# A hybrid encoder layer on one core: weight sums a slot behind their loads, three tiles moved off A's place, one hand-written order for stages 3 to 5

## The chip, the core and the metric

The kernel runs on one core of a Trainium2 chip. The core has TensorE (PE, matrix products; PEld is its weight load), VectorE (DVE), ScalarE (ACT), GpSimd (POOL) and SyncE (SP), which here only issues DMAs; POOL issues DMAs too, beside arithmetic. The metric is the device time in microseconds of one execution; lower is better.

## What is computed

One layer over a prompt of 2048 tokens and a sample of 64 tokens, 1024 features, all in 32-bit floats:

```python
def trunk_layer(x, mk, mv, conv_buf, C0, n0, m0, ff_buf, p):
    y, conv_new, C, n, m = token_mixer(rms_norm(x, p['norm_mix_pre']), conv_buf, C0, n0, m0, ...)
    x = x + rms_norm(y, p['norm_mix_post'])
    y = memory_attend(rms_norm(x, p['norm_mem_pre']), mk, mv, p['w_mq'], p['w_mo'])
    x = x + rms_norm(y, p['norm_mem_post'])
    y, ff_new = conv_ffn(rms_norm(x, p['norm_ffn_pre']), ff_buf, p['w_up'], p['ffn_conv_w'], p['w_down'])
    x = x + rms_norm(y, p['norm_ffn_post'])
    return x, conv_new, C, n, m, ff_new

def memory_attend(xn, mk, mv, w_q, w_o):          # 4 heads of 256, 256 memory tokens
    q = (xn @ w_q).reshape(B, T, MEM_HEADS, MEM_HD)
    s = jnp.einsum('bthd,bmhd->bhtm', q, mk) * (MEM_HD ** -0.5)
    o = jnp.einsum('bhtm,bmhd->bthd', jax.nn.softmax(s, axis=-1), mv).reshape(B, T, D_MODEL)
    return o @ w_o

def conv_ffn(xn, ff_buf, w_up, ffn_conv_w, w_down):   # d_ff = 2816
    up, ff_new = causal_dwconv(xn @ w_up, ff_buf, ffn_conv_w)
    a, g = jnp.split(up, 2, axis=-1)
    return (jax.nn.gelu(g) * a) @ w_down, ff_new
```

`token_mixer` is one input projection, a gated short convolution beside an mLSTM with four heads, and one output projection.

## The kernel before

The kernel splits each 32-bit matrix into a high and a low half (`split`, L102 on ScalarE and L103 on VectorE; `split_g`, L108 and L109, the same with a gain) and makes each product of three matrix products (`mm3`, L116 to L118). `self.dma` (L72) issues on SP, `self.store` (L75) on POOL. Five stages follow one another:

- Stage 1 makes the input projection, stage 2 the mLSTM and the output projection. For each 128 tokens, `post` (L558 to L568) takes the norm of the result, adds the residual from the tile `xt2` and stores the row as `x1d` from one of two tiles `yn2`. Those three tiles and `cn`, the mLSTM's memory, lie in the pool `p2w`.
- Stage 3 is the attention. First a fold: it multiplies the query weights with the memory's keys (products `pA`) and the memory's values with the output weights (`pB`), which gives the matrices A and B, each as two halves; their pools take the place that stage 2's pools leave. Then come 16 chunks of 128 tokens: transposes of `x1` (L1073), scores, softmax, output, `post`, which stores `x2d`, and `x2_T`, which transposes the normed result for stage 4 (L1229). Beside that `sums` prepares stage 4's weights in 44 slots: a slot loads four pieces of `w_up` of 128 KB into a tile `sums` (three buffers, shared with other raw loads), makes four additions or subtractions on VectorE (L1141 to L1144) and stores the tile as `wsd` with 512 KB. Slots are called at up to three points per chunk.
- Stage 4 is the up projection with its convolution and gate, 3 passes of 22 units, in a scheme that saves one product in eight with the sums of the weights; the result goes to memory as `hd`.
- Stage 5 is the down projection. The 2816 rows of weights are taken in six parts (`PARTS`), and each part goes through all tokens in blocks of 256: load `hr<-hd`, split to `hh` (two buffers each), products `y`, addition to `acc` (L1580). In the last part, the norm and the residual `xt<-x2d` (L562 to L568) follow the additions of each chunk of 128, and two stores `out_y` of 256 KB from SP. There a chunk's L568 and its stores come only after the squares of the next chunk (`hold`).

Where nothing is said, a scheduler sets each engine's order from the program's order and its own estimates; `manual_schedule` takes an engine out of this and gives it the program's order. Before, PE was so ordered in all stages, SP in the chunks of stage 3 and in stage 4, ACT, DVE and POOL in the fold and in the last part of stage 5. SP in stage 5 was the scheduler's. All DMAs that an engine issues stand in its row in one order: what stands behind one that waits, waits too.

Of the kernel before, what the change touches and what calls it, by code (L numbers as in the profile page):

```python
# [7 lines left out]
F32 = mybir.dt.float32  # L8
F32R = mybir.dt.float32r
AF = mybir.ActivationFunctionType  # L10
ALU = mybir.AluOpType
# [3 lines left out]
P = 128  # L15
D = 1024
# [17 lines left out]
NB = 352  # L34
NPASS = T // (2 * NB)
PARTS = [3, 3, 4, 4, 4, 4]
CG = dict(mix=0, mem=8, kv=16, ffn=24, mnw=32, cw=36, fw=48)
# [29 lines left out]
class Prog:  # L67
# [68 lines left out]
    def build(self):  # L136
        tc, nc = self.tc, self.nc
        with ExitStack() as es:
# [41 lines left out]
            self.phase2()  # L180
            self.phase3()
            self.phase4()
            self.phase5()

# [543 lines left out]
    def phase2(self):  # L728
        tc, nc, a = self.tc, self.nc, self.a
        V = nc.vector  # L730
        with ExitStack() as es:
# [11 lines left out]
            wk.tile([P, 16], F32, name="padw")  # L743
            yns = [wp.tile([P, D], F32, name="yn2%d" % i) for i in range(2)]
            gb = wp.tile([P, D], F32, name="gb2")
            xt_ = wp.tile([P, D], F32, name="xt2")
            wo1 = wp.tile([P, 2, 4, D], F32R, name="wo1")
            wo = lambda part, k, sl: (self.wo0(part, k) if k < 4 else wo1[:, part, k - 4])[:, sl]
            cn = {16: wp.tile([P, H, VW], F32, name="cn_s"), 0: wp.tile([P, H, VW], F32, name="cn_p")}

# [227 lines left out]
    def phase3(self):  # L978
# [8 lines left out]
        with ExitStack() as es:  # L987
            es.enter_context(tc.manual_schedule(engines={self.pe}))
            py_ = self.pool(es, "p3py", bufs=3, space=PSUM)
            with ExitStack() as es0:  # L990
                zw = self.wop.tile([P, 7168], F32R, tag="w", name="zw")
                raw4 = self.wop.tile([P, D], F32, tag="w7", name="raw4")
# [62 lines left out]

            es.enter_context(tc.manual_schedule(engines={mybir.EngineType.SP}))
            zq = self.zq = self.pool(self.qes, "zq", side="right")
# [72 lines left out]
            def sums():  # L1130

                KH = KT // 2
                for f in range(NF):
                    for q in range(2):
                        t = self.rawp.tile([P, 4, 2 * P], F32, tag="raw", name="sums", bufs=3)
                        for i, j in ((0, f), (1, NF + f)):
                            src = a["w_up"][j].rearrange("p (two k) c -> p two k c", two=2)[:, :, 2 * q:2 * q + 2]
                            for h in range(2):
                                self.dma(t[:, i + 2 * h], src[:, h].rearrange("p k c -> p (k c)"))
                        a11, a21, a12, a22 = (t[:, i] for i in range(4))  # L1140
                        V.tensor_tensor(out=a22, in0=a21, in1=a22, op=ALU.add)  # L1141
                        V.tensor_tensor(out=a21, in0=a11, in1=a21, op=ALU.subtract)
                        V.tensor_tensor(out=a11, in0=a22, in1=a11, op=ALU.subtract)
                        V.tensor_tensor(out=a12, in0=a12, in1=a11, op=ALU.subtract)  # L1144
                        self.store(self.wsd[f, :, :, q * 2 * P:(q + 1) * 2 * P], t)
                        yield
# [88 lines left out]
    def phase4(self):  # L1235
# [14 lines left out]
        with ExitStack() as es:  # L1250
            es.enter_context(tc.manual_schedule(engines={self.pe, mybir.EngineType.SP}))
            left = self.pool(es, "p4l")
# [47 lines left out]
            def w_split(w, n):  # L1300
                if w is None:
                    return
                if n == "wd":
                    o = left.tile([P, 2, KH, P], F32R, tag="wd", name="wd", bufs=1)
                else:
                    o = first.pop(n, None)
                    if o is None:
                        o = w_op(n, 2 if n == "wc" else 1)
                self.split(o[:, 0], o[:, 1], w.r[n])
                w.o[n] = o  # L1310
# [102 lines left out]
            w = w_load(0, ("wb",), tk.w)  # L1413
            w_split(w, "wa")
            t_split(0, tk, "B11", tk.r["R11"])
            t_split(0, tk, "B21", tk.r["R21"])
            v = head1(0, w, tk.o)
            t_adds(tk)
            t_split(0, tk, "T2", tk.X)
            w_split(w, "wb")  # L1420
# [78 lines left out]
    def phase5(self):  # L1499
        tc, nc, a = self.tc, self.nc, self.a  # L1500
        V = nc.vector
        with ExitStack() as es:
            es.enter_context(tc.manual_schedule(engines={self.pe}))
            ac0 = self.pool(es, "p5a")
# [38 lines left out]
            def need(i):  # L1543
                if i < len(work) and i not in hs:
                    pi, t0 = work[i]
                    hs[i] = load_h(f0s[pi], PARTS[pi], t0)
            ws = {0: load_down(0, 0, PARTS[0])}
            need(0)
            held = None
            tail = None  # L1550
            for i, (pi, t0) in enumerate(work):
                last = pi == len(PARTS) - 1
                if t0 == groups[3] and pi + 1 < len(PARTS):
                    ws[pi + 1] = load_down(pi + 1, f0s[pi + 1], PARTS[pi + 1])
                if i == len(PARTS):
# [4 lines left out]
                need(i)  # L1560
                need(i + 1)
                h = hs.pop(i)
                for j in range(t0 // P, (t0 + min(2 * P, T - t0) + P - 1) // P):
# [117 lines left out]
```

## Time and profile before

| | us |
|---|---|
| median of 3 runs (lowest, highest) | 2924.99 (2923.73, 2928.92) |
| the profiled execution | 2930.46 |
| its span, first to last instruction | 2928.8 |
| granted clock of TensorE, mean of the span | 0.99 |
| busy: TensorE, VectorE, ScalarE, GpSimd | 2839.5, 1718.0, 1205.7, 383.4 |

Stage 2 ends at about 1009 us of the span, the fold at 1071, the chunks at 1492, stage 4 at 2409; the last part of stage 5 begins at about 2830. In the rows below, all times are from the start of the span. A row of a timeline has start, duration, engine, line, operation, output and inputs with their shapes, the count, and in brackets the idle time before it with what ended that. SPq and POOL rows with DMA_DIRECT2D are issues of transfers, not the transfers.

### The profile page before, as it was taken

How to read it: one execution, taken by the hardware profiler on the slowest of the kernel's cores; microseconds unless marked ns; L12 is line 12 of the kernel's file. 1: busy time of each engine (PE TensorE's matmuls, PEld its weight loads, DVE VectorE, ACT ScalarE, POOL GpSimd, SP SyncE). 2: the span in 40 equal slices, each digit the busy share in tenths (PEclk: the TensorE clock that was granted, in tenths of full speed). 3: DMA queues.
4: the chain of work that ended last, by engine and by line, in shares of the span. 5: the costliest groups of instructions: out<-in, count | busy, mean ns of one | idle time of the engine just before them, and what ended most of it. 6: DMA issues, size and time to landing. Idle time of an engine off the chain costs nothing.

```text
span 2928.8 us, 41744 instructions
## 1 busy us (share of the span) xinstructions
PE 2839.5 (97%) x15906; PEld 2625.9 (90%) x15906; DVE 1718.0 (59%) x2815; ACT 1205.7 (41%) x2463; POOL 383.4 (13%) x608
## 2 busy tenths in 40 slices
PE   8999999999999999999979999999999999999998
PEld 8999999998888877778769999999999988888887
DVE  6413422355666565566567778877887772534459
ACT  5224223233444353332345656566666654101113
POOL 1111011112212111222100000000000000000026
PEclk9999999999999999999989999999999999999999
DMA  8434332147676344677456454654454543322126
GB/s 279 149 100 126 106 114 91 60 150 268 217 223 220 101 145 135 219 235 252 158 183 216 153 174 136 218 173 153 151 181 156 175 132 102 96 62 81 58 79 214
DMA packets 211498, 456.84 MB, mean 156 GB/s; under 512 B 25414, under 2 KB 113672, under 8 KB 211298
## 3 DMA queue, kind: packets, MB, share of 16 engines
q1 hardware_dynamic: 180418, 346.14, 37.6%
q0 software_dynamic: 28720, 100.17, 9.0%
q10 hardware_dynamic: 2160, 7.87, 0.9%
q8 instruction: 125, 2.05, 0.3%
q14 instruction: 75, 0.61, 0.1%
HBM read 345.56 MB, written 108.54 MB: 155 GB/s over the span
## 4 chain that ended last, share of the span: by engine, by line
PE 51%; DVE 6%; DMA 3%; issue 2%; SPq 1%; ACT 1%; POOL 0%; DVEq 0%; POOLq 0%; ACTq 0%
PE up L116 10%; PE up L118 10%; PE up L117 10%; PE y L117 4%; PE y L118 4%; PE y L116 4%; DMA sums<-in_w_up 3%; DVE acc L568 1%; SPq L72 1%; PE yo L116 1%; PE yo L117 1%; PE yo L118 1%; PE sc L116 1%; PE sc L118 1%; PE sc L117 1%
## 5 line engine op out<-in xcount | busy, mean ns | idle before, releaser
L116 PE MATMUL y<-dh,hh 128*128 128x512 f32 x704 | 275.0, 391 | 5.1 <-ACT dh L102 5.1
L117 PE MATMUL y<-dl,hh 128*128 128x512 f32 x704 | 274.8, 390 | 2.4 <-DVE dl L103 2.4
L118 PE MATMUL y<-dh,hh 128*128 128x512 f32 x704 | 274.8, 390 | 0.0
L116 PE MATMUL mm<-xs,wh 128*128 128x384 f32 (+2 forms) x768 | 249.1, 325 | 9.6 <-ACT xs L108 7.3
L118 PE MATMUL mm<-xs,wl 128*128 128x384 f32 (+2 forms) x768 | 248.5, 324 | 1.6 <-DVE wl L103 1.6
L117 PE MATMUL mm<-xs,wh 128*128 128x384 f32 (+2 forms) x768 | 248.8, 324 | 0.0
L1580 DVE TENSOR_TENSOR acc<-y,acc 128x512 f32<-128x512 f32 x170 | 115.5, 689 | 181.3 <-PE y L118 180.5
L116 PE MATMUL up<-B,wa 128*128 128x352 f32 x528 | 172.4, 326 | 8.8 <-ACT wa L102 8.8
L116 PE MATMUL up<-T,wb 128*128 128x352 f32 x528 | 172.1, 326 | 3.8 <-ACT wb L102 3.2
L116 PE MATMUL mmb<-bh,xs 128*128 128x384 f32 (+1 forms) x512 | 173.4, 339 | 0.0
L118 PE MATMUL up<-B,wa 128*128 128x352 f32 x528 | 170.1, 322 | 3.2 <-DVE wa L103 3.2
L118 PE MATMUL mmb<-bh,xs 128*128 128x384 f32 (+1 forms) x512 | 172.5, 337 | 0.0
L117 PE MATMUL mmb<-bl,xs 128*128 128x384 f32 (+1 forms) x512 | 172.4, 337 | 0.0
L117 PE MATMUL up<-T,wb 128*128 128x352 f32 x528 | 170.4, 323 | 1.7 <-DVE T L103 1.7
L117 PE MATMUL up<-B,wa 128*128 128x352 f32 x528 | 170.4, 323 | 0.1
L118 PE MATMUL up<-T,wb 128*128 128x352 f32 x528 | 169.8, 322 | 0.5 <-DVE wb L103 0.5
L116 PEld LDWEIGHTS y<-dh,hh 128*128 128x128 f32 x704 | 132.7, 188 | 33.0 <-ACT dh L102 5.4
L117 PEld LDWEIGHTS y<-dl,hh 128*128 128x128 f32 x704 | 132.6, 188 | 30.4 <-DVE dl L103 3.1
L75 POOL DMA_DIRECT2D hd<-da x88 | 47.4, 541 | 851.4 <-DVE da L1482 823.1
L102 ACT CAST hh<-hr 128x1024 fp32r<-128x1024 f32 (+3 forms) x54 | 49.3, 914 | 263.8 <-PE y L118 262.7
L118 PEld LDWEIGHTS y<-dh,hh 128*128 128x128 f32 x704 | 132.6, 188 | 28.0 <-DVE hh L103 0.5
L116 PEld LDWEIGHTS mm<-xs,wh 128*128 128x128 f32 x768 | 145.5, 190 | 10.6 <-ACT xs L108 7.7
(462 smaller groups left out, 7869.0 us busy)
## 6 DMA issues: line engine op xcount, KB each, us to landing
ws<-wsd SPq DMA_DIRECT2D x132, 512.0 KB, 4.4
raw<-in_w_up SPq DMA_DIRECT2D x66, 512.0 KB, 5.5
raw<-in_wA SPq DMA_DIRECT2D x47, 512.0 KB, 3.6
sums<-in_w_up SPq DMA_DIRECT2D x176, 128.0 KB, 4.3
wsd<-sums POOLq DMA_DIRECT2D x44, 512.0 KB, 4.0
wr<-in_w_up SPq DMA_DIRECT2D x66, 256.0 KB, 4.6
xt<-in_x SPq DMA_DIRECT2D x32, 512.0 KB, 4.4
hr<-hd SPq DMA_DIRECT2D x32, 512.0 KB, 3.9
```

The costliest lines, as they stand in the source:

```text
L72: self.nc.sync.dma_start(out=out, in_=in_)
L75: self.nc.gpsimd.dma_start(out=out, in_=in_)
L102: nc.scalar.copy(hi, src)
L116: nc.tensor.matmul(out, lhsT=lh, rhs=rh, start=(first and i == 0), stop=False, skip_group_check=more)
L117: nc.tensor.matmul(out, lhsT=lh, rhs=rl, start=False, stop=False, skip_group_check=more)
L118: nc.tensor.matmul(out, lhsT=ll, rhs=rh, start=False, stop=(last and i == n - 1), skip_group_check=more)
L568: nc.vector.scalar_tensor_tensor(out=yn[:w, sl], in0=yn[:w, sl], scalar=r[:w, 0:1], in1=xt[:w, sl], op0=ALU.mult, op1=ALU.add)
L1580: V.tensor_tensor(out=acc[j][:, sl], in0=pt, in1=acc[j][:, sl], op=ALU.add)
```

## The change

Three things are changed. In `sums`, a slot's loads are issued ahead of the four additions and the store of the slot before (`made`). In stage 2, the tiles `yn2`, `xt2` and `cn` come from another pool, `p2m`. And the order by hand of PE and SP is one context, `self.ms`, from the chunks of stage 3 to the end of stage 5: SP in stage 5 now goes by the program's order, for which the loads of the first down weights stand behind the first `hr`, and those of the later parts behind the next `hr`. Two places, at the starts of stages 4 and 5, get a higher priority with the scheduler, and one split at the start of stage 4 is moved by a line.

```diff
+HEAD = 120
@@ build
-            self.phase3()
-            self.phase4()
-            self.phase5()
+            with ExitStack() as self.ms:
+                self.phase3()
+                self.phase4()
+                self.phase5()
@@ phase2
-            yns = [wp.tile([P, D], F32, name="yn2%d" % i) for i in range(2)]
+            yns = [l2.tile([P, D], F32, name="yn2%d" % i) for i in range(2)]
-            xt_ = wp.tile([P, D], F32, name="xt2")
+            xt_ = l2.tile([P, D], F32, name="xt2")
-            cn = {16: wp.tile([P, H, VW], F32, name="cn_s"), 0: wp.tile([P, H, VW], F32, name="cn_p")}
+            cn = {16: l2.tile([P, H, VW], F32, name="cn_s"), 0: l2.tile([P, H, VW], F32, name="cn_p")}
@@ phase3
-            es.enter_context(tc.manual_schedule(engines={self.pe}))
             with ExitStack() as es0:
+                es0.enter_context(tc.manual_schedule(engines={self.pe}))
...
-            es.enter_context(tc.manual_schedule(engines={mybir.EngineType.SP}))
+            self.ms.enter_context(tc.manual_schedule(engines={self.pe, mybir.EngineType.SP}))
...
             def sums():
+                def made(f, q, t):
+                    a11, a21, a12, a22 = (t[:, i] for i in range(4))
+                    V.tensor_tensor(out=a22, in0=a21, in1=a22, op=ALU.add)
+                    V.tensor_tensor(out=a21, in0=a11, in1=a21, op=ALU.subtract)
+                    V.tensor_tensor(out=a11, in0=a22, in1=a11, op=ALU.subtract)
+                    V.tensor_tensor(out=a12, in0=a12, in1=a11, op=ALU.subtract)
+                    self.store(self.wsd[f, :, :, q * 2 * P:(q + 1) * 2 * P], t)
+                last = None
                 for f in range(NF):
                     for q in range(2):
...
                                 self.dma(t[:, i + 2 * h], src[:, h].rearrange("p k c -> p (k c)"))
-                        a11, a21, a12, a22 = (t[:, i] for i in range(4))
-                        V.tensor_tensor(out=a22, in0=a21, in1=a22, op=ALU.add)
-                        V.tensor_tensor(out=a21, in0=a11, in1=a21, op=ALU.subtract)
-                        V.tensor_tensor(out=a11, in0=a22, in1=a11, op=ALU.subtract)
-                        V.tensor_tensor(out=a12, in0=a12, in1=a11, op=ALU.subtract)
-                        self.store(self.wsd[f, :, :, q * 2 * P:(q + 1) * 2 * P], t)
+                        if last is not None:
+                            made(*last)
+                        last = f, q, t
+                        if (f, q) == (NF - 1, 1):
+                            made(*last)
                         yield
@@ phase4
-            es.enter_context(tc.manual_schedule(engines={self.pe, mybir.EngineType.SP}))
...
-            w_split(w, "wa")
-            t_split(0, tk, "B11", tk.r["R11"])
+            with tc.high_priority(offset=HEAD):
+                w_split(w, "wa")
+                t_split(0, tk, "B11", tk.r["R11"])
+                t_adds(tk)
+                t_split(0, tk, "T2", tk.X)
+            v = head1(0, w, tk.o)
             t_split(0, tk, "B21", tk.r["R21"])
-            v = head1(0, w, tk.o)
-            t_adds(tk)
-            t_split(0, tk, "T2", tk.X)
@@ phase5
-            es.enter_context(tc.manual_schedule(engines={self.pe}))
...
-            ws = {0: load_down(0, 0, PARTS[0])}
-            need(0)
+            with tc.high_priority(offset=HEAD):
+                need(0)
+                ws = {0: load_down(0, 0, PARTS[0])}
...
-                if t0 == groups[3] and pi + 1 < len(PARTS):
-                    ws[pi + 1] = load_down(pi + 1, f0s[pi + 1], PARTS[pi + 1])
...
                 need(i)
                 need(i + 1)
+                if t0 == groups[3] and pi + 1 < len(PARTS):
+                    ws[pi + 1] = load_down(pi + 1, f0s[pi + 1], PARTS[pi + 1])
```

TensorE's order is the same before and after, in all its rows. Three places of the other engines follow; line numbers of the changed kernel are one to nine higher.

SP in the last part of stage 5, from the loads ahead of the first store on (`hr`: a block's input, `xt5`: a chunk's residual, `acc0`, `acc1`: the first and second chunk of block 0, and so on). Before:

```order
L72 DMA hr_25401<-hd_86 128x4x256
L72 DMA hr_25494<-hd_86 128x4x256
L72 DMA hr_25587<-hd_86 128x4x256
L72 DMA out_y<-fo5_25388 64x512 x2
L72 DMA xt5_25450<-x2d_97 128x1024
L72 DMA out_y<-acc0_22837 128x512 x2
L72 DMA xt5_25499<-x2d_97 128x1024
L72 DMA hr_25680<-hd_86 128x4x256
L72 DMA out_y<-acc1_22838 128x512 x2
```

And now:

```order
L73 DMA xt5_25400<-x2d_97 128x1024
L73 DMA out_y<-fo5_25382 64x512 x2
L73 DMA xt5_25444<-x2d_97 128x1024
L73 DMA out_y<-acc0_22831 128x512 x2
L73 DMA hr_25488<-hd_86 128x4x256
L73 DMA xt5_25493<-x2d_97 128x1024
L73 DMA out_y<-acc1_22832 128x512 x2
L73 DMA xt5_25537<-x2d_97 128x1024
L73 DMA out_y<-acc2_22833 128x512 x2
L73 DMA hr_25581<-hd_86 128x4x256
```

Before, the loads `hr` of blocks 1 to 3 stood ahead of the first store, and that of block 4 behind the stores of `acc0`; now it is that of block 2 which stands behind the stores of `acc0`, that of block 3 behind those of `acc2`, and so on to block 7.

VectorE in a chunk of stage 3, from the last of `post` to the reduction of the scores (the sums rows of one line are the same step of two slots: the L1144 row ends a slot, the next L1141 row begins the chunk's last one). Before:

```order
L1143 TENSOR_TENSOR sums<-sums 128x256
L94 TENSOR_SCALAR pov<-poss 128x1
L94 TENSOR_SCALAR rsv<-ss_11175 128x1
L1144 TENSOR_TENSOR sums<-sums 128x256
L568 SCALAR_TENSOR_TENSOR yn_10174<-yn_10174,por,xr 128x512 x2
L1101 TENSOR_SCALAR sm_11181<-rsr 128x1
L94 TENSOR_SCALAR r2v<-ss_11168 128x1
L1141 TENSOR_TENSOR sums<-sums 128x256
L1108 TENSOR_REDUCE sm_11181<-sc_11183 128x2
L1128 TENSOR_SCALAR xr<-yn_10174,r2r 128x1024
```

And now (L1136 to L1139 are the four steps):

```order
L95 TENSOR_SCALAR pov<-poss 128x1
L95 TENSOR_SCALAR rsv<-ss_11171 128x1
L1138 TENSOR_TENSOR sums<-sums 128x256
L570 SCALAR_TENSOR_TENSOR yn_10175<-yn_10175,por,xr 128x512 x2
L1103 TENSOR_SCALAR sm_11177<-rsr 128x1
L1139 TENSOR_TENSOR sums<-sums 128x256
L95 TENSOR_SCALAR r2v<-ss_11164 128x1
L1136 TENSOR_TENSOR sums<-sums 128x256
L1130 TENSOR_SCALAR xr<-yn_10175,r2r 128x1024
L1110 TENSOR_REDUCE sm_11177<-sc_11179 128x2
```

The last step of a slot moves from ahead of the two multiply-adds to behind them, and the scaling `xr` goes ahead of the reduction; the first step of the chunk's last slot keeps its place.

ScalarE at the start of stage 3, with each row's waits (DMASW: a transfer that POOL issued, DMAHW: one that SP or ScalarE issued). Before:

```order
L102 CAST ys<-py 128x512 [waits PE_49]
L558 ACTIVATE yn_6305,poss<-yo 128x512 [waits DMASW1_49,DVE_49,PE_49]
L558 ACTIVATE yn_6305,poss<-yo 128x512 [waits DVE_49,PE_49]
L108 ACTIVATE A<-pA,cst 128x256 [waits DMAHW4_49,DMASW4_49,DMAHW5_49,DMASW3_49,DMAHW6_49,DVE_49,PE_49]
L102 CAST zw<-raw 128x1024 [waits DMAHW4_49]
```

And now:

```order
L103 CAST ys<-py 128x512 [waits PE_49]
L560 ACTIVATE yn_6305,poss<-yo 128x512 [waits DMASW1_49,DVE_49,PE_49]
L560 ACTIVATE yn_6305,poss<-yo 128x512 [waits DVE_49,PE_49]
L109 ACTIVATE A<-pA,cst 128x256 [waits DMAHW5_49,DMAHW4_49,DMAHW6_49,DVE_49,PE_49]
L103 CAST zw<-raw 128x1024 [waits DMAHW4_49]
```

The two waits for POOL's transfers are gone from the first write of A; the first write of B, later in the same row, has three of that kind where it had one.

## Rows read from the trace of the kernel before

**Rows 1.** The page's first part: busy time, share of the span, instructions.
```profile
PE 2839.5 (97%) x15906; PEld 2625.9 (90%) x15906; DVE 1718.0 (59%) x2815; ACT 1205.7 (41%) x2463; POOL 383.4 (13%) x608
```
**Rows 2.** Waits of PE, 1009 to 2415: in total, times, longest.
```profile
PE tp L1229 <- DVE xs L103: 18.2, 8, 4.2
...
PE pA L116 <- DVE A L109: 6.5, 4, 4.1
```
**Rows 3.** Busy time per window: length, PE, PEld, DVE, ACT, POOL, PEclk, DMA.
```profile
2849.00:2860.00 11.00, 11.00 (x50) 9.12 (x49) 10.93 (x14) 3.83 (x9) 8.41 (x7) 1.00 0.79 239
```
**Rows 4.** Chain that ended last, 2830 to 2929, shares by line.
```profile
by line: DVE acc L568 35.6%; DVE acc L1580 21.2%; DVE poss L563 17.9%; issue 7.8%; DVE hh L103 2.8%; DVE fo L568 2.4%; DVE fo L134 1.2%; DVE acc L562 1.2%; ACT fo L133 1.1%; ACT hh L102 1.0%; ACT junk L558 1.0%; DVE pov L94 0.8%; PE y L128 
```
**Rows 5.** Timeline of DVE in the last part.
```profile
2844.74 2.45 DVE L568 SCALAR_TENSOR_TENSOR acc<-acc,por,xt 128x512 f32<-128x512 f32 x2
...
2848.47 1.23 DVE L103 TENSOR_TENSOR hh<-hr,hh 128x1024 fp32r<-128x1024 f32 x1
...
2859.46 1.23 DVE L103 TENSOR_TENSOR hh<-hr,hh 128x1024 fp32r<-128x1024 f32 x1
```
**Rows 6.** Timeline of SP's issues in the last part.
```profile
2845.51 2.05 SPq L72 DMA_DIRECT2D out_y<-acc  x2
2847.60 0.43 SPq L72 DMA_DIRECT2D xt<-x2d  x1
2849.72 0.38 SPq L72 DMA_DIRECT2D hr<-hd  x1
```
**Rows 7.** DMA issues, 2836 to 2925: count, KB each, median us to landing.
```profile
xt<-x2d SPq DMA_DIRECT2D x15, 512.0 KB, 3.7
hr<-hd SPq DMA_DIRECT2D x5, 512.0 KB, 4.2
```
**Rows 8.** Timeline of ACT in the last part: the cast ahead of a split.
```profile
2845.70 1.03 ACT L102 CAST hh<-hr 128x1024 fp32r<-128x1024 f32 x1
```
**Rows 9.** Timeline between stages 2 and 3: DVE, POOL, ACT, PE.
```profile
1011.17 1.42 DVE L568 SCALAR_TENSOR_TENSOR yn<-yn,por,xt 128x512 f32<-128x512 f32 x2 [0.75 <-POOL por L96]
1012.88 0.57 POOL L75 DMA_DIRECT2D x1d<-yn  x1 [1.75 <-DVE yn L568]
1016.03 0.47 ACT L108 ACTIVATE A<-pA,cst 128x256 fp32r<-128x256 f32 x1 [6.59 <-issue]
1016.53 0.48 DVE L109 SCALAR_TENSOR_TENSOR A<-pA,cst,A 128x256 fp32r<-128x256 f32 x1 [3.95 <-ACT A L108]
1017.07 0.58 PE L116 MATMUL pA<-mk,hi 128*128 128x256 f32 x1 [4.05 <-DVE A L109]
```
**Rows 10.** Busy time per window, as rows 3, just behind it.
```profile
1015.04:1021.87 6.83, 4.38 (x19) 4.08 (x19) 4.63 (x9) 5.03 (x10) 1.94 (x1) 0.50 0.27 92
```
**Rows 11.** Waits of DVE in the chunks of stage 3: total, times, longest.
```profile
DVE sums L1141 <- DMA sums<-in_w_up: 64.6, 30, 5.9
```
**Rows 12.** Timeline of one chunk of stage 3: POOL's issues, then DVE.
```profile
1196.40 0.70 POOL L75 DMA_DIRECT2D wsd<-sums  x1
...
1198.89 0.56 POOL L96 TENSOR_TENSOR r2r<-r2v,small 128x1 f32<-128x1 f32 x1 [0.66 <-DVE r2v L94]
...
1204.68 0.42 DVE L1141 TENSOR_TENSOR sums<-sums 128x256 f32<-128x256 f32 x1 [5.94 <-DMA sums<-in_w_up]
...
1205.63 0.74 DVE L1128 TENSOR_SCALAR xr<-yn,r2r 128x1024 f32<-128x1024 f32 x1
...
1209.50 1.28 DVE L103 TENSOR_TENSOR xs<-tp,xs 128x512 fp32r<-128x512 f32 x2
```
**Rows 13.** Stage 4 to 5: waits of PE from 2400 on, timelines of SP and ACT.
```profile
PE y L116 <- ACT dh L102: 5.1, 1, 5.1
PE y L117 <- DVE dl L103: 2.4, 1, 2.4
...
2404.44 0.96 SPq L72 DMA_DIRECT2D hr<-hd  x2
...
2413.05 2.94 ACT L102 CAST dh<-raw 128x1024 fp32r<-128x1024 f32 x3
```

More of the change, by code (lines that the diff above doesn't have):

```diff
@@ L1130, in sums @@
             def sums():
-                KH = KT // 2
+                def made(f, q, t):
[6 more added lines that the diff above has]
+                last = None
                 for f in range(NF):
```

## The prediction

> **What bounds the kernel now.** I read the page's engine table first [rows 1]: TensorE is busy for 97% of the span, so it has nothing to do for only 2928.8 - 2839.5 = 89 us, and a change that leaves its instructions alone (this one does: their order is the same, row for row) can win only there and where its clock is low. Next comes the list of what TensorE waited for, from the start of stage 3 to the end of stage 4 [rows 2]. The reader is to see two lines there: the fold at the start of stage 3 waits for the low half of A (6.5 us, of which 4.1 at once), and the transposes of `x2_T` wait for splits of VectorE (18.2 us in eight waits). Third, the end. There TensorE is not the bound, though it is as busy: in each of the seven stretches of 11 us from 2838 to 2915, of which one row stands for all, VectorE too is busy for 10.93 of 11.00 us, and ScalarE for less than 4 [rows 3], and the chain that ended last goes through VectorE's lines for nearly all of its length [rows 4]. So in the last 85 us or so whatever holds VectorE up is paid in full. All other stretches I leave out, since the change moves nothing there that stands on a chain.
>
> **The change part by part. Part 5, the tail.** VectorE's order in the last part was written out by hand before and is the same now: a block of 256 tokens is one split `hh<-hr` and two chunks of two additions, two final multiply-adds (L568) and a small sum [rows 5]. Split to split it took 10.99 us (2859.46 less 2848.47). What moved is SP. Before, SP sent the next load of `hr` as soon as the split had freed its buffer: in the rows, the split that starts at 2848.47 ends at 2849.70 and the load goes out at 2849.72, for use two blocks later [rows 5, 6]. Now loads 2 to 7 of this part, six of them, stand in SP's row behind the two stores of the block's first chunk, and those wait for that chunk's L568 on VectorE, which is the last thing but the small sum ahead of the very split that needs the load. So the load starts at the place where the rows have the `xt` load that follows the stores, 2847.60, in place of two blocks earlier. Nearest prices for its way: an `hr` load took 4.2 us to land in this stretch and an `xt` load of the same size, behind the same stores, 3.7 [rows 7]; I take 4.0, since now the `hr` is the one behind the stores. ScalarE's cast follows with 1.03 us [rows 8]. The split then starts at 2847.60 + 4.0 + 1.03, rounded up to 2852.7 for the step from cast to split, in place of 2848.47: **4.25 us a block**, 3.9 to 4.6 by the two rows and some contention. Behind the split, VectorE's additions, multiply-adds and the stores of the block all stand still, and behind those the next load. Nothing hides it, as VectorE had 0.07 us to spare in a stretch. Six blocks give **+25.5 us**; bounds 22 and 30.
> TensorE then pauses some 4.3 us a block. Pauses of that length brought its clock to half in this trace: after the 4.05 us pause that ended at 1017.07 the granted clock was 0.50, the lower of its two levels (1.2 GHz in place of 2.4), over a stretch of 6.83 us [rows 9, 10]. Half a clock over 6.83 us costs 3.4 us of work, and 11.0 [rows 3] + 3.4 = 14.4 still goes into a block of 11.0 + 4.25 = 15.25 us, so I put it at nothing; its cover is the stall itself, with 0.85 us to spare.
>
> **Part 2 to 3, the tiles.** Before, ScalarE's first write of A stood idle for 6.59 us, to 1016.03, and not for TensorE: the profile names no engine [rows 9]. A lay on the place of `yn2`, whose last store POOL issued at 1012.88. With the tiles elsewhere that wait leaves A's first write and falls on B's, some 25 us later, when the stores have long landed. The next thing late is VectorE, busy with L568 till 1011.17 + 1.42 = 1012.59; the low half of A starts there in place of 1016.53, and TensorE's pause of 4.05 us shrinks to about 0.1. If the half clock of 1015.04 to 1021.87 goes too, another 4.38 / 2 = 2.2 us are won [rows 10]; against it, later loads in the fold move along only in part. I take **-4.5**, bounds -2 and -7.
>
> **Stage 3, the sums.** In the program text a slot's four additions now stand behind the next slot's loads. But VectorE is not ordered by hand there, and its rows show the additions where they were: the first addition of the chunk's last slot still stands ahead of the scaling `xr`, the reduction and the split that TensorE waits for. Before, this addition waited 5.94 us, to 1204.68, for a load of which SP could issue the first piece only when the buffer was free [rows 11, 12]; the split then came at 1209.50. SP's row is as it was. What does change is POOL: the store of the slot before (issued at 1196.40 [rows 12]) now goes out behind the `x2d` store and behind `r2r` (1198.89), so 0.5 MB less competes with the load that is waited for. That may bring it 0 to 1.5 us earlier in some of the eight or so chunks with a wait; the reduction moves behind the scaling, which costs 0.74 us where that chain ends last. I take **-2**, with half of the 18.2 as one bound (-9) and seven times 0.74 as the other (+5).
>
> **Stage 4 to 5.** The first `hr` now goes ahead of the three loads of down weights, which stood in stage 4's loads before. TensorE's pauses there were 5.1 and 2.4 us, for ScalarE's and VectorE's halves of the weights [rows 13]; those casts stand behind stage 4's last activations on ScalarE in both orders. SP could issue from 2404.44 on and the first cast of a weight came at 2413.05, which leaves 8.6 us for loads that land in some 4 [rows 7, 13]. I take **+0.5**, bounds 0 and +2. The priority around the start of stage 4 moves no row: 0.
>
> **Sum.** 25.5 - 4.5 - 2 + 0.5 = +19.5 us. The profiled execution took 2930.46 us (span 2928.8), so it would take 2949.96; it stands 5.47 above the median of the runs, 2924.99, and on that median the forecast is **2944.5 us**.
>
> **A rule against the change.** The clock at half over 6.83 us is what rows 10 show. The Trainium skill, "TensorE: Matmul & The Clock Gate", section "HAM oscillation — how this bites in real kernels", goes further: a kernel whose matrix products stop for a load in each tile falls back to half rate in every tile. [...]
>
> **The rivals.**
> (a) The additions really lag. If the waits for the sums' loads vanish with the change, the 18.2 us of the transposes go too: 2944.5 - 16.2 (beyond the 2 already taken) = 2928.3, within 0.2%. For it: the program's text. Against it: VectorE's rows. 7%.
> (b) The clock decides the tail. If every pause brings the clock to half for the whole block, TensorE's 11.0 us of work become 22 and it is the bound: 6 x 11 = 66 in place of 25.5, 2985. For it: the half clock behind pauses of 4 us. Against it: it was 6.83 us long [rows 10], not 15. 4%.
> (c) Faster: the load is hidden after all. The mechanism is SP's row: if the `hr` load were issued before the stores' wait ends, or if VectorE's split had 4.25 us of slack, the tail costs nothing and the two gains stay: 2924.99 - 6 = 2919. It decides from a stall of under 1 us a block on. For it: only that loads ran two blocks ahead before. Against it: rows 3 and 5, where VectorE has no slack, and SP's rows. 6%.
> (d) The stall is paid back by contention. L568 took 2.45 us in the tail but 1.42 with POOL idle at 1011.17 [rows 5, 9], and the small sum waits too; if the stall drew POOL's work and VectorE's apart, up to 2 us a chunk would come back, 4 a block: about 2921. Against it: POOL's multiplication hangs on the additions of the same chunk, which move with it. 3%. The Trainium skill, "SBUF — State Buffer", section "SBUF: two separate sides", says that these two engines share a pair of ports as an exclusive lock, for which the one that comes second waits out the other's whole instruction; the longer L568 agrees with that, and the rule would make (d) possible, not likely.
>
> **How the numbers follow.** The forecast's own case holds 80%, with 2931 to 2957 as its range: the low end has the tail at 22, the tiles at -7 and the sums at -9, the high end the tail at 30, the sums at +5 and the tiles at -2, and the start of stage 5 at +2, which would be 2960; all four at their worst at once are not needed, so I stop at 2957. The range reaches down to rival (a) and leaves out (b), (c) and (d): 2927 to 2957. A difference of 0.2% is 5.85 us, about what a measurement can tell from none. Faster by more: (c) and (d), 0.08 or so; within: (a) and the low end of the forecast's case, 0.09; slower: the rest, 0.83.
>
> **What would show it.** In the profile of the changed kernel: in the tail, a VectorE idle time of about 4 us ahead of six splits `hh<-hr`, ended by ScalarE's cast, and SP's `hr` right behind two `out_y`; splits 15.2 us apart; TensorE with a pause per block. Between stages 2 and 3, ScalarE's first A at about 1010 to 1012 and no pause of 4 us. In stage 3, waits for the sums' loads that are still near 60 us in all. Wrong it is if the splits stay 11 us apart, or if the waits for `x2_T`'s transposes vanish.

## The result, and the profile after

The changed kernel takes **2947.7 us** (median of 4 runs, 2940.63 to 2948.53) against 2924.36 for the kernel before on the same chip (4 runs, 2923.6 to 2928.92). The ratio is 1.0071, with a 95% interval of 1.0052 to 1.009: slower by 20.8 us (15 to 26). The ratio goes by all runs and not by the two medians, which lie 23.3 us apart. The forecast was 2944.5, or 19.5 slower, in a range of 2927 to 2957.

The profiled execution took 2947.28 us, its span 2945.6, which is 16.8 longer than before. Where these come from is read from the first and last products of each stage on TensorE in the two traces:

| stretch | before, us | after, us | difference |
|---|---|---|---|
| start to the first product `pA` of the fold | 1008.55 | 1006.25 | -2.3 |
| fold, first `pA` to end of the last `pB` | 61.37 | 55.58 | -5.8 |
| chunks of stage 3, to the end of the last `yo` | 422.45 | 417.21 | -5.2 |
| stage 4, to the end of the last `up` | 916.65 | 916.46 | -0.2 |
| stage 5, to the end of the span | 519.74 | 550.07 | +30.3 |

**The tail.** These are VectorE's waits of the changed kernel from 2826 to 2942 (in total, times, longest):

```profile
DVE hh L104 <- ACT hh L103: 29.7, 6, 5.1
DVE acc L570 <- POOL por L97: 0.7, 1, 0.7
```

Before, the longest wait of this kind in the last part was 0.4 us; now six of 4.7 to 5.1 us hold 29.7 of the 30.3 us. One of them, in the timelines of VectorE, SP and ScalarE:

```profile
2847.30 2.44 DVE L570 SCALAR_TENSOR_TENSOR acc<-acc,por,xt 128x512 f32<-128x512 f32 x2
...
2850.94 0.16 DVE L95 TENSOR_SCALAR pov<-poss 128x1 f32<-128x1 f32 x1
2856.14 1.23 DVE L104 TENSOR_TENSOR hh<-hr,hh 128x1024 fp32r<-128x1024 f32 x1 [5.04 <-ACT hh L103]
...
2872.28 1.22 DVE L104 TENSOR_TENSOR hh<-hr,hh 128x1024 fp32r<-128x1024 f32 x1 [5.09 <-ACT hh L103]
...
2848.07 2.04 SPq L73 DMA_DIRECT2D out_y<-acc  x2
2850.20 0.39 SPq L73 DMA_DIRECT2D hr<-hd  x1
2850.67 0.51 SPq L73 DMA_DIRECT2D xt<-x2d  x1
...
2855.06 1.04 ACT L103 CAST hh<-hr 128x1024 fp32r<-128x1024 f32 x1 [6.70 <-DMA hr<-hd]
```

The reader is to follow the times: the two stores wait for L570 (L568 before) and go out from 2848.07, the `hr` load at 2850.20, the cast starts when it has landed, at 2855.06, and the split at 2856.14. VectorE had been free from 2851.10. Splits are 16.1 us apart (2872.28 less 2856.14) where [rows 5] had 10.99. In between, all of the block's work takes what it took: L570 has 2.44 us, as in [rows 5].

The issues of this stretch, to set against [rows 7]:

```profile
xt<-x2d SPq DMA_DIRECT2D x15, 512.0 KB, 3.8
out_y<-acc SPq DMA_DIRECT2D x30, 256.0 KB, 2.3
hr<-hd SPq DMA_DIRECT2D x6, 512.0 KB, 4.7
```

And the chain that ended last, from 2825 on, against [rows 4]; a transfer now holds 23% of it, where no transfer was on the chain before:

```profile
by line: DVE acc L570 29.0%; DMA hr<-hd 23.2%; DVE acc L1589 16.9%; DVE poss L565 8.8%; issue 8.4%; ACT hh L103 5.2%; DVE fo L570 2.0%; SPq L73 1.8%; DVE acc L564 1.0%; DVEq L1686 0.5%; POOLq L1686 0.5%; DVE pov L95 0.4%; DVE hh L104 0.2%; 
```

TensorE now pauses ahead of each block, for 2.4 to 4.1 us in five of the six and 0.3 us in the first, and its clock falls. Two windows of one block each (columns as [rows 3]):

```profile
2840.00:2856.10 16.10, 11.46 (x48) 8.86 (x48) 10.98 (x13) 3.95 (x10) 7.51 (x6) 1.00 0.51 163
2856.10:2872.20 16.10, 12.90 (x48) 9.68 (x48) 10.98 (x13) 3.89 (x10) 7.52 (x6) 0.89 0.52 163
```

VectorE does the same 10.98 us of work in 16.1. In the second window the granted clock is 0.89 in the mean, since from 2856.41 to 2859.82, behind the pause, it was 0.50, the lower of its two levels; TensorE's work grows from 11 to 12.9 us and still fits.

**The fold.** The timeline at its start, against [rows 9]:

```profile
1008.87 1.42 DVE L570 SCALAR_TENSOR_TENSOR yn<-yn,por,xt 128x512 f32<-128x512 f32 x2 [0.75 <-POOL por L97]
1010.20 0.48 DVE L110 SCALAR_TENSOR_TENSOR A<-pA,cst,A 128x256 fp32r<-128x256 f32 x1
...
1007.94 0.47 ACT L109 ACTIVATE A<-pA,cst 128x256 fp32r<-128x256 f32 x1 [0.81 <-PE pA L119]
...
1012.26 0.38 PE L117 MATMUL pA<-mk,hi 128*128 128x256 f32 x1 [0.55 <-DVE A L110]
```

ScalarE now waits 0.81 us, and for TensorE's products; before it waited 6.59 with no engine named. VectorE's half of A follows directly on L570. TensorE's pause is 0.55 us in place of 4.05, and the clock stays up (1.00 from 1005 to 1020, where [rows 10] had 0.50).

**Stage 3 and the change to stage 5.** TensorE's waits from 1000 to 2409, against [rows 2, 13]:

```profile
PE tp L1238 <- DVE xs L104: 15.3, 9, 4.2
...
PE y L117 <- ACT dh L103: 5.1, 1, 5.1
...
PE pA L117 <- DVE A L110: 2.5, 3, 1.3
PE y L118 <- DVE dl L104: 2.4, 1, 2.4
```

The transposes' waits went from 18.2 to 15.3, and those at the start of stage 5 are the same to the tenth. This pair of traces alone says little of the sums: `tiles_only` below, with the old sums, has 15.9.

### The profile page after: what moved, and what is told of

Same layout as the page of the kernel before. It is cut to its first block, busy times and chain, and to the rows that moved or that the text cites. A ratio compares the mean times of both kernels' runs of the same rounds, so it can differ in the third digit from the quotient of the medians.

```text
span 2945.6 us, 41739 instructions
## 1 busy us (share of the span) xinstructions
PE 2846.5 (97%) x15906; PEld 2628.0 (89%) x15906; DVE 1716.3 (58%) x2815; ACT 1206.6 (41%) x2463; POOL 378.0 (13%) x608
## 4 chain that ended last, share of the span: by engine, by line
PE 51%; DVE 6%; DMA 4%; issue 2%; ACT 1%; SPq 1%; POOL 0%; DVEq 0%; POOLq 0%; ACTq 0%
PE up L117 10%; PE up L119 10%; PE up L118 10%; PE y L118 4%; PE y L119 4%; PE y L117 4%; DMA sums<-in_w_up 2%; DVE acc L570 1%; PE yo L117 1%; PE yo L118 1%; PE yo L119 1%; DMA hr<-hd 1%; PE sc L119 1%; PE sc L117 1%; PE sc L118 1%
## 5 line engine op out<-in xcount | busy, mean ns | idle before, releaser
L117 PE MATMUL y<-dh,hh 128*128 128x512 f32 x704 | 278.9, 396 | 20.5 <-ACT hh L103 15.4
L119 PE MATMUL y<-dh,hh 128*128 128x512 f32 x704 | 278.7, 396 | 2.4 <-DVE hh L104 2.3
```

The lines of the kernel that those rows point to most:

```text
L117: nc.tensor.matmul(out, lhsT=lh, rhs=rh, start=(first and i == 0), stop=False, skip_group_check=more)
L119: nc.tensor.matmul(out, lhsT=ll, rhs=rh, start=False, stop=(last and i == n - 1), skip_group_check=more)
```

## The experiments

The theory: the loss is SP's order in the last part alone, where a load stands behind stores that wait for VectorE; the two other edits win. Each run has its own runs of the kernel before beside it, and its ratio is to those. The rivals: the loss needs the weights' loads, the priorities or the clock; the gain of stage 3 is only a matter of when it begins, or one of VectorE's order.

### One part undone, and each part alone

`sp5_auto` leaves SP in stage 5 to the scheduler again:

```diff
             with ExitStack() as self.ms:
                 self.phase3()
                 self.phase4()
-                self.phase5()
+            self.phase5()
@@ phase5
+            es.enter_context(tc.manual_schedule(engines={self.pe}))
```

> The changed kernel, with SP in stage 5 left to the scheduler again (TensorE alone by hand there), so that the loads hr run two blocks ahead of their use as before. Theory: the six waits of 5.0 us of VectorE ahead of its splits come from SP's order alone, so some 30 us of the last part go: 2947.7 - 30 = about 2917.5, faster than the kernel before by 6 to 8 us, splits 11.0 us apart. Rival (the new place of the weights' loads, the priorities or a clock that falls make the loss): 2935 or more.

Measured: 2910.98 us, ratio 0.9946 (0.9933 to 0.9959). Splits are 10.99 us apart again, with no wait ahead of them:

```profile
2831.12 1.23 DVE L104 TENSOR_TENSOR hh<-hr,hh 128x1024 fp32r<-128x1024 f32 x1
...
2842.11 1.23 DVE L104 TENSOR_TENSOR hh<-hr,hh 128x1024 fp32r<-128x1024 f32 x1
```

The theory holds, and the time is lower than expected: the rest of the change wins 16 us and not 7.

`sp5_only` is the kernel before with `phase5` of the changed one and SP by hand in it:

```diff
-            es.enter_context(tc.manual_schedule(engines={self.pe}))
+            es.enter_context(tc.manual_schedule(engines={self.pe, mybir.EngineType.SP}))
```

> The kernel before with stage 5 alone as changed: SP by the program's order there, the weights' loads behind the next hr. Theory: the loss is all of this part: 2924.4 + 30 = about 2954.5 (2950 to 2957). Rival (the loss needs the earlier stages' changes too): under 2945.

Measured: 2954.84 us, ratio 1.0093 (1.0078 to 1.0108), so +27 us (23 to 32). Its stage 5 takes 549.4 us by the trace, 29.7 more than before, with six waits of 4.7 to 5.4 us ahead of the splits (and one of 0.2):

```profile
DVE hh L104 <- ACT hh L103: 29.9, 7, 5.4
```

The loss is of this part, alone.

`tiles_only` moves the three tiles and nothing else:

```diff
-            yns = [wp.tile([P, D], F32, name="yn2%d" % i) for i in range(2)]
+            yns = [l2.tile([P, D], F32, name="yn2%d" % i) for i in range(2)]
...
```

> The kernel before with the tiles yn2, xt2 and cn in the other pool alone. Theory: the fold starts about 4 us earlier and the low clock behind its pause goes: 5.4 us less, and the 2.7 us by which stage 2 was early in the changed kernel may be of this part too: 2924.4 - 5.4 = 2919 (2916 to 2920). Rival (the 5 us that the chunks of stage 3 won are of this part too, since a moved fold shifts what the loads meet): 2912 to 2914.

Measured: 2916.31 us, ratio 0.9968 (0.9956 to 0.998), -9.4 us (6 to 13). The fold takes 55.5 us, as in the changed kernel, so -5.9 is of the fold; the chunks take 421.0, as before. The rival falls. What is left of the 9.4 lies ahead of the fold, and there runs differ: to the first `pA` the four profiled kernels with the tiles in the old place took 1005.7 to 1008.6 us, the eight with them in the new one 1000.4 to 1008.0. Whether the tiles win there too stays open.

`sums_only` takes the new `sums` alone, with `made` as in the diff of the change:

```diff
-                        a11, a21, a12, a22 = (t[:, i] for i in range(4))
...
-                        self.store(self.wsd[f, :, :, q * 2 * P:(q + 1) * 2 * P], t)
+                        if last is not None:
+                            made(*last)
+                        last = f, q, t
+                        if (f, q) == (NF - 1, 1):
+                            made(*last)
```

> The kernel before with the sums' additions a slot behind their loads alone; VectorE's and GpSimd's rows of stage 3 are those of the changed kernel. Theory: the store of a chunk's second last slot goes out later and the load that is waited for lands earlier, so the chunks win the 5 us that they won in the changed kernel: about 2919.5 (2918 to 2922). Rival (those 5 us were a matter of when the chunks began): 2924, no change.

Measured: 2920.41 us, ratio 0.9972 (0.9963 to 0.9982), -8.2 us (5 to 11). The chunks take 409.2 us where the three kernels with the old sums and the old stores took 419.9 to 422.5, and TensorE's wait is

```profile
PE tp L1236 <- DVE xs L103: 9.7, 8, 4.8
```

in place of 18.2. The gain is there without the moved tiles. Of the 13.2 us between this trace's chunks and those of the kernel before, 8.5 are that wait, and 3.6 are TensorE's busy time for the same products, 397.4 us and not 401.0, since with fewer pauses its granted clock was 0.99 in the mean and not 0.98. This profiled run is the fastest of its nine; in the five other profiled kernels with the new sums and VectorE left to the scheduler, the chunks took 410.8 to 417.2 us, and the most in the changed kernel.

### What it is in the sums that wins

The additions did not lag: in the changed kernel's rows the last slot's first addition still waits, ahead of the scaling and the reduction (chunk at 1186; VectorE, GpSimd and SP, against [rows 12]):

```profile
1195.10 0.42 DVE L1136 TENSOR_TENSOR sums<-sums 128x256 f32<-128x256 f32 x1 [5.49 <-DMA sums<-in_w_up]
1195.44 0.75 DVE L1130 TENSOR_SCALAR xr<-yn,r2r 128x1024 f32<-128x1024 f32 x1
1196.10 0.68 DVE L1110 TENSOR_REDUCE sm<-sc 128x2 f32<-128x512 f32 x1
...
1188.54 0.59 POOL L76 DMA_DIRECT2D x2d<-yn  x1 [1.23 <-DVE sm L1103]
1189.77 0.56 POOL L97 TENSOR_TENSOR r2r<-r2v,small 128x1 f32<-128x1 f32 x1 [0.64 <-DVE r2v L95]
1190.29 0.71 POOL L76 DMA_DIRECT2D wsd<-sums  x1
...
1186.85 2.18 SPq L73 DMA_DIRECT2D sums<-in_w_up  x4
```

The load that is waited for, in four pieces, goes out from 1186.85 here. The store of the slot before is issued 3.4 us behind that, and behind `x2d`. In the kernel before, SP's row of the load is

```profile
1195.54 3.83 SPq L72 DMA_DIRECT2D sums<-in_w_up  x4
```

and the store went out at 1196.40 [rows 12], 0.9 us behind its start. Either this or VectorE's new order could be the cause. `store_sp` keeps VectorE's and ScalarE's rows of before, and moves nine stores alone:

```diff
+                late = None
                 for f in range(NF):
                     for q in range(2):
...
+                        if late is not None:
+                            self.dma(*late)
+                            late = None
...
-                        self.store(self.wsd[f, :, :, q * 2 * P:(q + 1) * 2 * P], t)
+                        if (2 * f + q) % 4 == 1 and 2 * f + q > 8:
+                            late = self.wsd[f, :, :, q * 2 * P:(q + 1) * 2 * P], t
+                        else:
+                            self.store(self.wsd[f, :, :, q * 2 * P:(q + 1) * 2 * P], t)
```

> The kernel before with nine stores alone moved: the store of every fourth slot of the sums, from the tenth on, is issued by SP behind the next slot's loads and not by GpSimd ahead of or beside them. VectorE's and ScalarE's rows are those of before. Theory: the 8 us of the run with the sums alone changed came from these stores no longer running beside the load that VectorE waits for; that load (7.5 us from first issue to landing before, 6.5 to 7.0 changed) lands 0.7 us or more earlier and the time falls by 5 to 9 us (ratio 0.997 to 0.998). Rival (the gain was VectorE's order, with the last addition behind the multiply-adds and the scaling ahead of the reduction): no change, 0.999 to 1.001.

Measured: 2916.35 us, ratio 0.9976 (0.9967 to 0.9985), -7.0 us (4 to 10). TensorE's waits of the transposes, and VectorE's of the loads, from 1055 to 1480:

```profile
PE tp L1236 <- DVE xs L103: 7.6, 3, 4.7
```
```profile
DVE sums L1145 <- DMA sums<-in_w_up: 53.5, 31, 6.0
```

[Rows 2, 11] had 18.2 and 64.6. Over the nine loads of this kind, the mean way from first issue to landing was 7.6 us before, 7.5 in `sp5_only` and 7.3 in `tiles_only`; 7.0 in the changed kernel, 6.8 in `sp5_auto` and 6.5 in `sums_only`; 6.2 here. So moving these stores is enough for the gain, with VectorE's order as before. How far they moved can be read from the issues of the same nine. Against the first piece of the load, the store went out 0.9 to 2.2 us later in the three kernels with the old sums, which is about when the last piece did; 3.4 to 5.1 later with the new sums; and 2.0 to 3.7 later here. The last piece's own way to landing was 5.2 to 5.4 us in the mean in the first three, 4.5 to 4.8 with the new sums and 4.3 here. Here the store also goes out from SP and not from GpSimd, and whether the later place or the other engine did it is not told apart.

`dve_hand` asks what a real lag would be worth. It is `hr_ahead` (below) with VectorE too by hand in the chunks, in the program's order:

```diff
+            es.enter_context(tc.manual_schedule(engines={mybir.EngineType.DVE}))
             zq = self.zq = self.pool(self.qes, "zq", side="right")
```

> The kernel of the run before this one, with VectorE too ordered by hand in the chunks of stage 3, so that the additions of a slot really come a slot behind its loads and no longer ahead of the scaling and the first reduction. Theory: in the changed kernel the additions did not lag, and the 12 to 15 us that TensorE waits ahead of the transposes of x2_T are mostly theirs; they fall under 5 us and the time to 2899 to 2904. Rival (the program's order puts additions between the two reductions of the scores and holds up the softmax): TensorE waits elsewhere, 2911 or more.

Measured: 2942.92 us, ratio 1.0066 (1.0053 to 1.0079). The chunks take 445.7 us. The first waits of TensorE and of VectorE there:

```profile
PE tp L1239 <- DVE xs L104: 36.1, 13, 9.4
```
```profile
DVE sm L1118 <- ACT pp L1116: 44.8, 32, 3.2
DVE sums L1137 <- DMA sums<-in_w_up: 41.5, 13, 4.8
```

The loads are waited for less (41.5 against 60.8 us in the changed kernel, in 13 places against 27), but VectorE now stands 32 times for the softmax's exponentials (44.8 us against 13.8), and the split that TensorE waits for stands behind both. The rival holds. It says that the program's order as it stands is no good order for VectorE, not that a lag by itself is worth nothing: a lag in an otherwise equal order was not tried.

### What it takes to mend the tail

`hr_ahead` keeps the changed kernel's one order by hand, and issues the load of block i+2 at the start of block i of the last part (`load_hr` is the first half of `load_h`, the tile and its DMA):

```diff
                 need(i + 1)
+                if last and i + 2 < len(work):
+                    pj, tj = work[i + 2]
+                    hrs[i + 2] = load_hr(f0s[pj], PARTS[pj], tj)
@@ need
-                    hs[i] = load_h(f0s[pi], PARTS[pi], t0)
+                    hs[i] = load_h(f0s[pi], PARTS[pi], t0, hrs.pop(i, None))
```

> The changed kernel with its one order by hand kept, and in the last part the load hr of block i+2 issued at the start of block i in place of block i+1. Theory: a load needs only to stand one block further ahead of its split, whoever sets SP's order; the six waits of 5.0 us go and the time is that of the kernel with SP left to the scheduler, about 2911 (ratio to before 0.993 to 0.997), splits 11.0 us apart. Rival (SP's order by hand costs elsewhere in stage 5 too): 2917 or more.

Measured: 2906.05 us, ratio 0.9933 (0.992 to 0.9945) to the kernel before: faster than both kernels, by 19.6 us (16 to 23) than before. Two splits of its tail, and a window (columns as [rows 3]):

```profile
2835.03 1.23 DVE L104 TENSOR_TENSOR hh<-hr,hh 128x1024 fp32r<-128x1024 f32 x1
...
2846.03 1.23 DVE L104 TENSOR_TENSOR hh<-hr,hh 128x1024 fp32r<-128x1024 f32 x1
```
```profile
2835.00:2846.00 11.00, 11.00 (x50) 9.12 (x49) 10.93 (x14) 3.84 (x9) 8.39 (x6) 1.00 0.72 240
```

The loads take 4.3 to 4.9 us to land here as well; they only start a block earlier. Stage 5 takes 520.0 us, where the kernel before took 519.7: one load's place in one queue is the whole of the 30 us.

`best_sp` joins `hr_ahead` with the sums of `store_sp`:

> The kernel with the hr loads a block further ahead and the tiles moved, with the sums of the run with nine stores moved to SP in place of the lagging additions. Theory: both ways keep the store away from the load that is waited for, and the gains do not add: within 0.1% of the kernel with the hr loads ahead, 2903 to 2909 (ratio 0.992 to 0.995). Rival (by SP is better, since its wait of TensorE was 7.6 us against 10.7): 2900 or less.

Measured: 2915.59 us, ratio 0.9953 (0.994 to 0.9967). It does not beat `hr_ahead` (their intervals touch), so the two ways to keep the store off do not add, as the theory had it, if at a ratio a little above its range. The traces say the same: the chunks took 410.7 us here and 411.2 in `hr_ahead`, and the two profiled runs differ ahead of the fold (1008.0 against 1000.6 us to the first `pA`), where like kernels differ too. Its edit is the two diffs above, with the old place of the additions.

### Why the load took longer than forecast

An `hr` took 4.7 us to land in the tail and not 4.0. Two more kernels ask why, with a single execution each, so their times count for little and their traces are read. `xt_behind` issues each chunk's `xt` behind the stores:

```diff
                         xt = ld.tile([P, D], F32, tag="xt", name="xt5", bufs=2)
-                        self.dma(xt[:w], self.x2[j * P:j * P + w])
...
                         held = [f]
+                        self.dma(xt[:w], self.x2[j * P:j * P + w])
```

> The changed kernel with the load xt of each chunk of the last part issued behind the two stores that follow it, so that no load goes out 0.5 us behind an hr. Theory: an hr took 4.7 us to land in the changed kernel and not 4.2 as before or the 4.0 that was forecast since the xt right behind it shares its way; it lands in 4.0 to 4.2 and VectorE's waits fall from 5.0 to about 4.4 us. Rival (the two stores ahead of it slow it): 4.7, waits of 5.0 us.

Measured: 2955.73 us, the `hr` at 4.8. It decides nothing: with this edit the `xt` goes out 0.5 us ahead of the `hr`, so the two still ran together, and the `xt`, now late, made new waits of VectorE (12.4 us in five), while those ahead of the six splits rose to 40.8 us. `xt_pairs` puts the loads `xt` a block ahead, in pairs and in four buffers, so that nothing goes out shortly behind an `hr`:

```diff
+                        if j not in xts:
+                            load_xt(j)
+                        if s == P and i + 1 < len(work):
+                            load_xt(j + 1)
+                            load_xt(j + 2)
+                        xt = xts.pop(j)
```

> The changed kernel with the loads xt of the last part in pairs, a block ahead, in four buffers: behind an hr stand only the two stores of the block's second chunk, which wait for VectorE, so nothing goes out within 0.5 us behind it (the two stores ahead of it stay). Theory: the xt sent 0.5 us behind the hr takes a part of its way; an hr lands in 4.0 to 4.2 us and not in 4.7, and VectorE's waits ahead of the splits fall from 5.0 to 4.3 to 4.5. Rival (the stores ahead of it slow it): 4.7, waits of 5.0 us.

Measured: 2943.25 us, and

```profile
hr<-hd SPq DMA_DIRECT2D x6, 512.0 KB, 4.4
```
```profile
DVE hh L104 <- ACT hh L103: 29.5, 6, 5.9
```

Four of the six waits are 4.5 to 4.7 us where the changed kernel had 4.7 to 5.1 and the theory 4.3 to 4.5, but two are 5.4 and 5.9, and the sum is that of the changed kernel. Part of the 0.7 us seems to be the `xt`; the rest is not settled.

## Why the prediction was right, point by point

- **The tail (+25.5 forecast, +30.3 in stage 5 by the trace).** The step was right in its mechanism and in its count, six waits; `sp5_only` shows it alone, `sp5_auto` and `hr_ahead` take it away in two ways. The size was off in one term, the load's way: I took 4.0 between the 4.2 of the `hr` row and the 3.7 of the `xt` row, and it was 4.7, or 4.4 to 4.8 one by one. That is 0.7 of the 0.8 us a block by which 30.3 / 6 = 5.05 exceeds 4.25; the splits came 16.1 us apart and not 15.2, and the term ended just above its own upper bound of 30. The `hr` row alone would have given 4.45 a block, or +26.7.
- **The clock in the tail (0 forecast).** Right. It fell, in five blocks of six, for 3.4 us each, where I had allowed for 6.83, and it cost nothing. (The 6.83 us of [rows 10] began 2 us before the pause ended, so they did not hold 6.83 us of work either.) Rival (b) falls by the windows: TensorE had 12.9 us of work in a block of 16.1. The Trainium skill's page "TensorE: Matmul & The Clock Gate", section "HAM oscillation — how this bites in real kernels", says that a kernel whose products stop for a load in each tile starts every tile at half rate; the trace agrees as far as the fall goes, in five blocks of six. The half rate did not last for the block, as (b) had it, and the 1.9 us or so that it added to TensorE's 11.0 stayed inside the wait for VectorE.
- **The tiles (-4.5 forecast, -5.8 in the fold).** Right, with the low clock gone too, as the bound of -7 allowed. In the eight profiled kernels with the tiles moved the fold took 55.5 to 55.6 us, in the four without 61.4 to 62.0.
- **The sums (-2 forecast; -5.2 in the changed kernel's trace, -8.2 alone).** That the additions would not move, and that the later store would shorten the load, was right; the size was wrong by a factor of two and a half to four, though both are inside the bounds. (In the trace of `sums_only` the chunks alone won 13.2, beyond the bound of -9.) I gave the store "0 to 1.5 us" in some chunks, and the nine loads did land 0.6 us sooner in the changed kernel and 1.1 in `sums_only`; but I charged the reduction's later place against it, and left out that with less waiting TensorE's clock stays up longer. `store_sp` shows that moving the stores alone carries the gain. Rival (a) falls: VectorE still waited 60.8 us for the loads.
- **Stage 4 to 5 (+0.5 forecast).** Both waits are unchanged, 5.1 and 2.4: 0.
- **Rivals (c) and (d)** fall by VectorE's rows: six waits of 5 us, and L570 at 2.44 us as before, so nothing of GpSimd's work drew apart.

The total came out close because two errors cancel: the tail cost 5 us more than forecast, the tiles and the sums won 4.5 more in that trace. That it lies 1 us from the forecast is luck; the sign is not, since the tail's 30 us are more than the other parts won in any trace here. What is not settled: the three parts alone add to -9.4 - 8.2 + 27.2 = +10 us, with some 6 us of uncertainty, the change as a whole measured +21 (15 to 26). The runs of the parts stand against another set of runs of the kernel before (2928.19 in the median, against 2924.36), and stretches 1 and 3 of the table differ by a few us from profile to profile of like kernels: the changed kernel's chunks, 417.2 us, are the longest of the six with these sums.

## What to carry to other kernels

When an engine's DMA queue goes from a scheduler's order to the program's, read that queue's new row for each load that now stands behind a store: the store's wait for the computing engine becomes the load's, and where the same engine needs the load next, each turn of the loop pays the load's whole way, as the 5 us a block did here. The load's place, one turn earlier, cures that; a return to the scheduler's order did as well here (0.9946 against 0.9933, with intervals that meet). And a wait for a load can be shortened by what else is sent at that moment: moving nine stores behind the load's last piece was worth as much here (-7.0 us) as the whole edit of the sums (-8.2).

## What the runs showed of the hardware

- Four loads of 128 KB took 7.3 to 7.6 us in the mean from first issue to last landing when GpSimd issued a store of 512 KB 0.9 to 2.2 us behind the first of them (three traces); 6.5 to 7.0 with the store 3.4 to 5.1 us behind; 6.2 with the store 2.0 to 3.7 us behind, from the queue of the loads.
- The same `hr` load, in the kernel before and in `sp5_auto`, landed in 3.7 to 3.9 us ahead of the last part's stores and in 4.2 to 4.6 among them; right behind two stores, as in the changed kernel and `sp5_only`, it took 4.3 to 5.2.
- Behind the five pauses of 2.4 to 4.1 us in the changed kernel's tail, TensorE's granted clock was 0.50, the lower of its two levels, for 3.4 us each; in `sp5_only` it was so behind three pauses of 3.7 to 4.0 us and not behind two of 2.1 and 2.3; around the end of the 4.05 us pause at the fold of the kernel before, it was so for 6.83 us.
